# Eight experts' weights streamed through TensorE on one core: another order of the experts, four more places for weights, another tail

## The chip, the cores and the metric

The kernel runs on one core of a Trainium2 chip. The metric is the device time of one execution in microseconds (us). Everything is computed and stored in 32-bit floating point; the weights come from the chip's memory in that form.

## What is computed

Two transformer blocks over 256 tokens of width 1024. The change touches the last layer of the second block: a mixture of experts (each token goes to 2 of 8 SwiGLU experts, whose hidden width is 3584), and the gate behind it (PLE below, after its names in the code).

```python
def swiglu(x, w1, w3, w2):
    return (jax.nn.silu(x @ w1) * (x @ w3)) @ w2

def moe_swiglu(x, router_w, w1, w3, w2):
    logits = (xt @ router_w).astype(jnp.float32)
    top_vals, top_idx = lax.top_k(logits, TOP_K)
    gates = jax.nn.softmax(top_vals, axis=-1)
    ...
    for e in range(N_EXPERTS):
        out = out + combine[:, e:e + 1] * swiglu(xt, w1[e], w3[e], w2[e])

# the last layer
h = h + moe_swiglu(f, router_w[j], moe_w1[j], moe_w3[j], moe_w2[j])
gate = jax.nn.sigmoid(rmsnorm(h, ple_norm_g[i]) @ ple_gate_w[i])
h = h + gate * (p[i] @ ple_proj_w[i])
```

## The kernel before

**Steps.** An expert's hidden width is cut into four chunks, 1024, 1024, 1024 and 512 (CHUNKS, L33). A *step* is one expert and one chunk: the products with w1 and w3 of this step, and then the product with w2 of the step before, whose hidden values are ready by then. STEPS (L49) is the order of the 32 steps: experts 0 and 4 take turns chunk by chunk, then 1 and 5, 2 and 6, 3 and 7. The order is written out when the program is built; all engines follow it.

**The stream of weights** (_Stream, from L62). All matrices of the stage are cut into parts of 128 x 1024 numbers (512 KB), 24 for a full step, 12 for one of the short last chunk, 672 in all; then two parts of p's projection and eight of the gate's matrix (pg). SyncE sends a part (L89) as soon as a slot is free. There are 32 lasting slots: 8 (RAW), 8 tiles that the dense layers used for split weights (wh, wl), 6 (MORE) and 10 (EARLY). Seven more tiles (two x, then xl, xh, xl, x and gain) take one part each while they wait for their own use: load_parts. Parts of p and pg are split into a high and a low half first (split, L311 to L322: ScalarE the high half, VectorE or GpSimd the low one), and at most four split parts are live at a time (advance).

**A matrix on TensorE** (wide, from L1470). Each expert has room for its first 64 tokens, 32 more and 32 more. The product of the first 64 (mm for w1, s for w3, o for w2) goes over the parts as they come. The two others stand behind branches on the number of the expert's tokens (`If` at L1492, over 64, and L1495, over 96). They run as `rest`, put off until the first part of the *next* matrix is done (catch_up), and only after them all parts of the matrix are given back:

```python
            for j, _ in parts:
                self.ws.release(j)
            take(1)
        for i, (j, (k0, k1, _, _)) in enumerate(parts):
            if i == 1:
                self.catch_up()
```

With these inputs expert 1 has over 96 tokens, expert 2 between 65 and 96, the others 64 or fewer.

**Between the products.** At fixed parts of w1 and w3 stand: the transposes of the hidden values of the step before (hidden), the gather of the next expert's tokens (gather), and, for an expert that has just ended, its way back to the tokens' order (way_back) and the sum into h, weighted by the gates (scatter, with a branch at L1589 and the sum on VectorE at L1593).

**The tail.** experts() ends with: w2 of (3, 3), way_back and scatter of expert 3, hidden of (7, 3), way_back of expert 7, w2 of (7, 3). moe() then plays the product of p with its projection (ple_value, four groups) and scatters expert 7 between them, transposes the normed sum, and comes to a branch for experts with over 128 tokens (overflow, L1664 to L1666: all engines load the largest number and compare it). Behind it stands the gate's product with pg in two halves, and the output.

Of the kernel before, what the change touches and what calls it, by code (L numbers as in the profile page):

```python
# [48 lines left out]
STEPS = [(e, c) for e0 in range(NE // 2) for c in range(NC) for e in (e0, e0 + NE // 2)]  # L49
# [13 lines left out]
class _Stream:  # L63
# [3 lines left out]
    def __init__(self, net, plan):  # L67
        self.net, self.plan = net, plan
        self.parts = [(i, q, s) for i, c in enumerate(plan) for q, s in enumerate(c[4])]
        self.raw, self.got = {}, {}  # L70
        self.loaded = self.opened = self.cut = self.used = self.cur = self.first = self.live = 0
        self.slots, self.cap = [(net.wp, "raw", RAW)] * RAW, RAW
        self.extra, self.hold = set(), False

        self.last, self.keep = sum(len(c[4]) for c in plan[-3:]), None
# [29 lines left out]
    def load_parts(self, tiles):  # L105

        for tile in tiles:
            assert self.loaded == self.opened + self.cap
            self.extra.add(self.loaded)
# [3 lines left out]
    def open(self, u):  # L113
        self.opened += 1
        self.cap -= u in self.extra
        self.load()

    def advance(self, n=PARTS):
        stop = self.cut + n
        while self.cut < stop and self.cut < len(self.parts) and self.live < PARTS:  # L120
            u = self.cut
            if u not in self.raw or self.whole(u):
# [3 lines left out]
            f = self.net.split_pair if len(self.plan[i][4]) == 1 else lambda v: self.net.split(v, j)  # L126
# [71 lines left out]
class _Net:  # L198
# [112 lines left out]
    def split(self, v, j=0):  # L311

        k, n = v.shape[1], v.shape[2]
        wh = self.t(self.wp, [P, 1024], "wh", F32R, bufs=PARTS)[:, : k * n].rearrange("p (k n) -> p k n", k=k)
        wl = self.t(self.wp, [P, 1024], "wl", F32R, bufs=PARTS)[:, : k * n].rearrange("p (k n) -> p k n", k=k)
# [1043 lines left out]
    def ple_value(self, i, xs, pp):  # L1359

        out = self.banks("mm")
        order = [(0, 0), (1, 0), (0, 1), (1, 1)]
# [173 lines left out]
    def hidden(self, sp, s, n):  # L1536


        g = self.t(sp, [P, 2, 4, P], "sw_g")
# [7 lines left out]
    def down(self, key, ys, g, n, many, first):  # L1547
# [15 lines left out]
        self.wide(key, y, lhs, 512, many, take)  # L1563
# [4 lines left out]
    def scatter(self, t, e, back, ys, many=None):  # L1568

        ps = []  # L1570
        rows = [slice(SET * j, SET * j + SET) for j in range(2)]

        def first():
            ps[:] = [self.bank("tr") for _ in range(2)]
            for j in range(2):
                self.mm(ps[j], back[rows[j], 0, t * P : t * P + P], ys[rows[j], 0, :], start=True, stop=True, skip_group_check=True)

        def others():
            for i in range(2):
                for d in range(2):  # L1580
                    for j in range(2):
                        self.mm(ps[j][:, d * 256 : d * 256 + 256], back[rows[j], 1 + 2 * i + d, t * P : t * P + P],
                                ys[rows[j], 1, i * 256 : i * 256 + 256], start=False, stop=i == 1, skip_group_check=True)

        def second():
            if many is None:
                others()
            else:
                with self.tc.If(many() > SET):  # L1589
                    others()  # L1590
            for j in range(2):
                hv = self.h[:, t, j * 512 : j * 512 + 512]
                self.nc.vector.scalar_tensor_tensor(hv, ps[j], self.gates[:, t, e : e + 1], hv, ALU.mult, ALU.add)  # L1593
# [3 lines left out]
    def experts(self, sp, p):  # L1597
# [11 lines left out]

        def hidden(e, c, s):  # L1610
            gs[e, c] = self.hidden(sp, s, CHUNKS[c][1] // 2)

        def finish(e, c):
# [3 lines left out]
            self.down(("w2", e, c), ys[e], gs.pop((e, c)), CHUNKS[c][1] // 2, F(number, e), c == 0)  # L1617
            return e if c == NC - 1 else None

        for i, (e, c) in enumerate(STEPS):  # L1620
# [18 lines left out]
            if n < 512:  # L1639
                assert not late  # L1640
                mids = {k: mids.get(2 * k, []) + mids.get(2 * k + 1, []) for k in range(4)}
# [18 lines left out]
        return [f for t in range(NT) for f in self.scatter(t, x, back[x], ys[x], F(number, x))], pT  # L1660

    def overflow(self, sp, again):

        nc = self.nc  # L1664
        most = nc.values_load(self.most[0:1, 0:1], min_val=0, max_val=S)
# [32 lines left out]
    def route_join(self, gen):  # L1698
# [8 lines left out]
        self.stream.load_parts([t_(self.act, [P, D], "x", bufs=3) for _ in range(2)])  # L1707
# [38 lines left out]
        for tag in ("wh", "wl"):  # L1746
# [23 lines left out]
        self.stream.load_parts([t_(self.act, [P, D], tag, bufs=3) for tag in ("xl", "xh", "xl")]  # L1770
                               + [t_(self.act, [P, D], "x", bufs=3), t_(self.cst, [P, D], "gain")])
        self.next_gain()
# [42 lines left out]
    def moe(self, i):  # L1815
        sp = self.se
        p = self.ple_load(i, self.act, "x", 3)
        done, pT = self.experts(sp, p)
        pp = [self.t(self.act, [P, D], "x", bufs=3) for t in range(NT)]
        value = self.ple_value(i, pT, pp)  # L1820
        x0, *x0T = (self.t(self.qp, [P, D], "raw", bufs=EARLY) for _ in range(3))
        x0T = [x.bitcast(F32R).rearrange("p (k n) -> p k n", k=KD) for x in x0T]
        self.play(value, n=2)
        done[0]()
        done[1]()
# [117 lines left out]
```

## Time and profile before

| | us |
|---|---|
| runs | 1774.54, 1767.98, 1769.01 |
| median | 1769.01 |
| the profiled execution | 1774.91 |
| its span, first to last instruction | 1773.1 |
| TensorE busy in the span | 1652.7 (93%) |
| VectorE busy | 671.5 (38%) |
| ScalarE busy | 514.1 (29%) |

The profile is that of one execution. PE is TensorE (PEld its loads of the stationary operand, PEq its sequencer), DVE VectorE, ACT ScalarE, POOL GpSimd, SP SyncE (SPq its DMA queue). Numbers behind L are lines of the kernel. TensorE's clock has two levels, 1.2 and 2.4 GHz; the granted clock is the share of the higher one. In brackets behind a row of the timeline stands the engine's idle time before it and what ended it.

### The profile page before, as it was taken

To read this page: it belongs to the slowest core of one execution; us is meant where nothing else is said; L and a number is where in the kernel's file an instruction comes from. 1 tells how busy PE (TensorE), PEld (TensorE's weight loads), DVE (VectorE), ACT (ScalarE), POOL (GpSimd) and SP (SyncE) were. 2 spreads that over 40 slices of the span, in tenths; PEclk is the share of its full clock that TensorE was granted. 3 is DMA by queue.
4 is the path that set the end of the run, shared out by engine and by line. 5 is a ranking of instruction groups with operands and counts; after the bars stand their busy time and mean duration, and the time that the engine had idled before them with its cause. 6 is when DMAs were issued, how large, how long until landed. Compare 5 with 4: busy or idle time off the path is not lost. (4 is left out here: it accounts for less than half of the span.)

```text
span 1773.1 us, 24424 instructions
## 1 busy us (share of the span) xinstructions
PE 1652.7 (93%) x9746; PEld 1014.6 (57%) x9749; DVE 671.5 (38%) x1132; ACT 514.1 (29%) x840; POOL 158.4 (9%) x152
## 2 busy tenths in 40 slices
PE   8999989999999999999997999999999998998867
PEld 6887768777888877784332534336433344333336
DVE  6656767576445587571110130101120111311134
ACT  5646646555444455551100100000000001000013
POOL 2001432510000013500000000000000000000011
PEclk9999999999999999999999999999999999998979
DMA  8654335545555558567999998999789999999951
GB/s 272 201 175 146 108 95 168 180 122 185 182 187 190 190 163 292 194 250 308 406 407 399 400 393 306 406 357 401 283 320 374 408 397 404 370 407 407 397 207 38
DMA packets 176117, 491.70 MB, mean 277 GB/s; under 512 B 16670, under 2 KB 21206, under 8 KB 175920
## 3 DMA queue, kind: packets, MB, share of 16 engines
q1 hardware_dynamic: 171376, 474.28, 72.1%
q0 software_dynamic: 4544, 14.52, 2.8%
q8 instruction: 157, 2.57, 0.6%
q14 instruction: 40, 0.33, 0.0%
HBM read 486.60 MB, written 2.14 MB: 276 GB/s over the span
## 5 line engine op out<-in xcount | busy, mean ns | idle before, releaser
L272 PE MATMUL mm<-wh,xh 128*128 128x512 f32 (+4 forms) x888 | 324.0, 432 | 7.1 <-PEq L1492 4.0
L320 DVE TENSOR_TENSOR wl<-raw,wh 128x1024 fp32r<-128x1024 f32 x211 | 266.7, 1275 | 130.8 <-ACT wh L316 120.4
L272 PE MATMUL mm<-wh,xl 128*128 128x512 f32 (+1 forms) x704 | 281.4, 400 | 0.7 <-DVE xl L491 0.5
L316 ACT CAST wh<-raw 128x1024 fp32r<-128x1024 f32 x228 | 237.5, 1051 | 143.8 <-PE mm L272 68.2
L272 PE MATMUL mm<-wl,xh 128*128 128x512 f32 (+3 forms) x924 | 254.1, 416 | 1.2 <-DVE wl L320 0.6
L272 PE MATMUL mm<-raw,xh 128*64 128x512 f32 (+3 forms) x1388 | 201.2, 467 | 20.7 <-PEq L1492 14.2
L272 PE MATMUL o<-raw,sw_g 128*64 128x512 f32 (+1 forms) x1268 | 195.5, 503 | 16.7 <-PEq L1492 9.7
L272 PE MATMUL s<-raw,xh 128*64 128x512 f32 (+3 forms) x1432 | 193.4, 457 | 16.5 <-PEq L1492 12.4
L1532 DVE TENSOR_TENSOR sw_s<-sw_s,s 128x512 f32<-128x512 f32 (+1 forms) x64 | 39.8, 621 | 405.9 <-PE s L272 367.6
L272 PEld LDWEIGHTS mm<-wh,xh 128*128 128x128 f32 (+2 forms) x888 | 145.7, 180 | 54.4 <-issue 10.6
L272 PEld LDWEIGHTS mm<-wl,xh 128*128 128x128 f32 (+2 forms) x924 | 145.1, 175 | 51.5 <-issue 10.1
L272 PEld LDWEIGHTS mm<-wh,xl 128*128 128x128 f32 x704 | 134.9, 192 | 29.8 <-DVE xl L491 2.5
L318 POOL TENSOR_TENSOR wl<-raw,wh 128x1024 fp32r<-128x1024 f32 x17 | 43.0, 2549 | 1198.4 <-ACT wh L316 1178.4
L272 PEld LDWEIGHTS s<-raw,xh 128*64 128x64 f32 (+1 forms) x1432 | 77.0, 125 | 124.2 <-issue 80.9
L1544 ACT COPY sw_g<-tr 128x512 f32<-128x512 f32 (+1 forms) x32 | 17.1, 533 | 446.9 <-PE tr L275 425.8
L272 PEld LDWEIGHTS o<-raw,sw_g 128*64 128x64 f32 (+1 forms) x1268 | 72.0, 126 | 128.8 <-issue 95.8
L272 PEld LDWEIGHTS mm<-raw,xh 128*64 128x64 f32 (+1 forms) x1388 | 72.3, 127 | 119.0 <-issue 91.8
L1557 DVE TENSOR_TENSOR xl<-xl,o 128x512 f32<-128x512 f32 x48 | 33.0, 686 | 163.3 <-PE o L272 137.2
L1530 ACT ACTIVATE sw_s<-mm 128x512 f32<-128x512 f32 (+1 forms) x64 | 34.8, 544 | 206.0 <-PE mm L272 167.8
L272 PE MATMUL o<-wh,sw_g 128*128 128x512 f32 (+2 forms) x256 | 61.0, 488 | 3.8 <-PEq L1492 2.2
L272 PE MATMUL s<-wh,xh 128*64 128x512 f32 (+6 forms) x236 | 51.0, 467 | 3.3 <-PEq L1492 2.6
L275 PEld LDWEIGHTS tr<-c_ident,sw_s 128*128 128x128 f32 x280 | 34.0, 151 | 32.8 <-issue 9.1
(363 smaller groups left out, 1606.7 us busy)
## 6 DMA issues: line engine op xcount, KB each, us to landing
raw<-in_moe_w_dram SPq DMA_DIRECT2D x504, 512.0 KB, 10.2
raw<-in_dense_w_dram SPq DMA_DIRECT2D x84, 512.0 KB, 4.5
wh<-in_moe_w_dram SPq DMA_DIRECT2D x81, 512.0 KB, 10.2
wl<-in_moe_w_dram SPq DMA_DIRECT2D x80, 512.0 KB, 10.2
raw<-in_w_in_dram SPq DMA_DIRECT2D x48, 512.0 KB, 4.6
raw<-in_nsa_w_in_dram SPq DMA_DIRECT2D x44, 512.0 KB, 5.1
raw<-in_w_o_dram SPq DMA_DIRECT2D x16, 512.0 KB, 4.8
raw<-in_ple_gate_w_dram SPq DMA_DIRECT2D x16, 512.0 KB, 5.0
```

What stands on the lines that cost most here:

```text
L272: self.nc.tensor.matmul(out, lhsT, rhs, start=start, stop=stop, **kw)
L275: self.nc.tensor.transpose(out, in_, self.ident if ident is None else ident)
L316: self.nc.scalar.copy(wh, v)
L318: self.nc.gpsimd.tensor_tensor(wl, v, wh.bitcast(F32), ALU.subtract)
L320: self.owed.append(lambda: self.nc.vector.tensor_sub(wl, v, wh.bitcast(F32)))
L1530: nc.scalar.activation(s[:, i, :n], ps[i][:, :n], AF.Silu)
L1532: nc.vector.tensor_mul(s[:, i, :n], s[:, i, :n], ps[i][:, :n])
L1544: copy(g[:, i, : n // P, :], ps[:, :n].rearrange("p (q n) -> p q n", n=P))
L1557: self.nc.vector.tensor_add(ys[:, i, :], ys[:, i, :], y[i])
```

## The change

The experts no longer go in pairs. Each begins when its predecessor is half through, in the order 0, 4, 1, 5, 2, 6, 3, 7: the steps are 0c0, 0c1, 4c0, 0c2, 4c1, 0c3, 1c0, 4c2, 1c1, 4c3, 5c0, 1c2, and so on to 7c0, 3c2, 7c1, 3c3, 7c2, 7c3. Four of the seven tiles that took one part (three x and gain) become lasting slots, 36 in all. For that, p gets a tile of its own, the gate's gain is loaded in the last step instead of at the routing, and the gain's tile leaves the slots 34 parts before the stream's end.

In the tail, way_back and scatter of expert 3 and way_back of expert 7 move into w1 and w3 of the last step, and hidden of (7, 3) into w2 of (7, 2); w2 of (7, 3) follows at once. The first group of p's product stands between that product and its catch_up. Expert 7 is scattered into four banks with one branch, and its sums stand between the groups of p and behind the transposes. The number for the overflow branch is loaded earlier. Behind that branch two parts of pg's first half and two of its second are split at once; six split parts may be live at the stream's end.

```diff
-STEPS = [(e, c) for e0 in range(NE // 2) for c in range(NC) for e in (e0, e0 + NE // 2)]
+ORDER = [e for e0 in range(NE // 2) for e in (e0, e0 + NE // 2)]
+STEPS = [(ORDER[i], c) for _, c, i in sorted((2 * i + c, c, i) for i in range(NE) for c in range(NC))]
...
-            if len(self.parts) - self.loaded <= self.last and slot[0] is not self.keep and slot[:2] != (self.net.wp, "raw"):
+            left = len(self.parts) - self.loaded
+            if left <= self.last and slot[:2] != (self.net.wp, "raw") or slot[0] is self.net.cst and left <= self.last + 24:
                 self.cap -= 1
                 continue
...
     def open(self, u):
         self.opened += 1
         self.cap -= u in self.extra
+        if u in self.become:
+            self.slots.insert(0, self.become[u])
         self.load()
...
+            end = len(self.parts) - u <= self.last
+            if self.live >= PARTS + 2 * end:
+                break
...
+        if more:
+            wh, wl = (self.t(self.qp, [P, 1024], "raw", bufs=EARLY).bitcast(F32R) for _ in range(2))
...
+    def spread(self, ps, t, back, ys):
+        for j in range(2):
+            r = slice(SET * j, SET * j + SET)
+            self.mm(ps[j], back[r, 0, t * P : t * P + P], ys[r, 0, :], start=True, stop=True, skip_group_check=True)
...
+            if i == len(STEPS) - 1:
+                late[3] = [F(turn_back, e)]
+                self.next_gain()
             self.up(("w1", e, c), xT[e], s, n, F(number, e), True, mids)
             self.up(("w3", e, c), xT[e], s, n, F(number, e), False, late)
-            done = finish(*prev[:2]) if prev is not None else None
+            if i < len(STEPS) - 1:
+                done = finish(*prev[:2]) if prev is not None else None
+            else:
+                finish(*prev[:2], {4: [F(hidden_last, e, c, s)]})
...
-        self.catch_up()
-        back[done], turn = self.way_back(sp, done)
-        turn()
-        hidden(*prev)
-        for t in range(NT):
-            for f in self.scatter(t, done, back[done], ys[done], F(number, done)):
-                f()
-        x = prev[0]
-        back[x], turn = self.way_back(sp, x)
-        turn()
-        finish(*prev[:2])
-        self.catch_up()
+        self.stream.wait()
+        self.stream.advance(2)
+        finish(*prev[:2])
+        self.stream.advance(4)
+        value = self.ple_value(1, pT, pp)
+        self.play(value, n=1)
+        self.catch_up()
+        self.sets.pop("s")
+        ps = [[self.bank(tag) for _ in range(2)] for tag in ("tr", "s")]
         for t in range(NT):
+            self.spread(ps[t], t, back[e], ys[e])
+        with self.tc.If(number(e) > SET):
+            for t in range(NT):
+                self.spread_rare(ps[t], t, back[e], ys[e])
...
-        p = self.ple_load(i, self.act, "x", 3)
+        p = self.ple_load(i, sp, "p")
...
+        most = self.nc.values_load(self.most[0:1, 0:1], min_val=0, max_val=S)
         done[0]()
+        self.scaled(0, x0, (0,))
+        self.play(value, n=1)
         done[1]()
-        self.scaled(0, x0)
+        self.scaled(0, x0, (1,))
         self.play(value, n=1)
-        done[2]()
-        done[3]()
         self.transposed(x0, x0T, 0, 4)
         self.play(value)
         self.transposed(x0, x0T, 4, 8)
-        self.overflow(sp, lambda: self.transposed(self.scaled(0, x0), x0T))
+        done[2]()
+        done[3]()
+        self.overflow(sp, most, lambda: self.transposed(self.scaled(0, x0), x0T))
+        self.stream.advance(4)
```

How the instructions of TensorE move is shown at three places. The first is the start of the seventh step, of the kernel before: behind the last part of w2 of the step before (o, from the hidden values sw_g) comes the first part of w1 (mm, from the tokens' tile xh), and then the branch for the tokens over 64. xh_6764 holds the tokens of expert 0.

```order
L272 MATMUL o_7223<-wl_8235,sw_g_8343 64x512 x2
L272 MATMUL o_7223<-raw_8237,sw_g_8343 64x512 x2
L272 MATMUL mm_6826<-raw_8324,xh_6764 64x256 x4
L1492 COMPARE_AND_BRANCH
L272 MATMUL o_7224<-wh_8223,sw_g_8343 32x256 x4
L272 MATMUL o_7224<-wh_8225,sw_g_8343 32x256 x4
L272 MATMUL o_7224<-wh_8227,sw_g_8343 32x256 x4
```

The same place in the changed kernel, where the lines have moved by 10 to 15 and xh_8265 holds the tokens of expert 1.

```order
L282 MATMUL o_7211<-raw_8133,sw_g_8353 64x512 x2
L282 MATMUL o_7211<-raw_8135,sw_g_8353 64x512 x2
L282 MATMUL mm_6820<-raw_8137,xh_8265 64x512 x2
L1507 COMPARE_AND_BRANCH
L282 MATMUL o_7212<-raw_8024,sw_g_8353 32x256 x4
L282 MATMUL o_7212<-raw_8026,sw_g_8353 32x256 x4
L282 MATMUL o_7212<-raw_8028,sw_g_8353 32x256 x4
```

The step in this place is the short last chunk of expert 0 before (64x256), and the first chunk of expert 1 now; before, expert 1 begins two steps later.

The second place is TensorE's work between w2 of (3, 3) and w2 of (7, 3) in the kernel before: the way back of expert 3 (tr from oh), hidden of (7, 3) (tr from sw_s), the scatter of expert 3 (tr from xl and back).

```order
L275 MATMUL tr_16792<-c_ident_86,oh_2308_16785 128x128 x2
L275 MATMUL tr_16791<-c_ident_86,oh_2308_16785 128x128 x4
L275 MATMUL tr_16803<-c_ident_86,sw_s_16480 128x128 x2
L275 MATMUL tr_16807<-c_ident_86,sw_s_16480 128x128 x2
L272 MATMUL tr_16811<-xl_14831,back_16790 128x512
L272 MATMUL tr_16812<-xl_14831,back_16790 128x512
L1589 COMPARE_AND_BRANCH
L272 MATMUL tr_16811<-xl_14831,back_16790 128x256
L272 MATMUL tr_16812<-xl_14831,back_16790 128x256
```

In the changed kernel these stand in w3 and w2 of the last step. The piece is w2 of (7, 2), with hidden of (7, 3) in its middle; its last row is the first part of w2 of (7, 3), from the tile that hidden has filled.

```order
L282 MATMUL o_7211<-raw_16259,sw_g_16514 64x512 x2
L282 MATMUL o_7211<-raw_16261,sw_g_16514 64x512 x2
L282 MATMUL o_7211<-raw_16263,sw_g_16514 64x512 x2
L285 MATMUL tr_16762<-c_ident_86,sw_s_16466 128x128 x2
L285 MATMUL tr_16766<-c_ident_86,sw_s_16466 128x128 x2
L282 MATMUL o_7211<-raw_16265,sw_g_16514 64x512 x2
L282 MATMUL o_7211<-raw_16267,sw_g_16514 64x512 x2
L282 MATMUL o_7211<-raw_16269,sw_g_16514 64x512 x2
L282 MATMUL o_7211<-raw_16364,sw_g_16514 64x512 x2
L282 MATMUL o_7211<-raw_16366,raw_16761 64x512 x2
L1507 COMPARE_AND_BRANCH
```

What stood alone between two products stands inside one now, and the first part of the last product follows with nothing between. The third place is what comes behind that product in the changed kernel: the rest of its parts, p's first group (mm from wh and wl), and only then the branch for tokens over 64.

```order
L282 MATMUL o_7211<-raw_16368,raw_16761 64x512 x2
L282 MATMUL o_7211<-raw_16370,raw_16761 64x512 x2
L282 MATMUL o_7211<-raw_16372,raw_16761 64x512 x2
L282 MATMUL mm_16885<-wh_16867,xh_16177 128x512
L282 MATMUL mm_16885<-wh_16867,xl_16178 128x512
L282 MATMUL mm_16885<-wh_16867,xh_16177 128x512
L282 MATMUL mm_16885<-wh_16867,xl_16178 128x512
L282 MATMUL mm_16885<-wl_16868,xh_16177 128x512 x2
L1507 COMPARE_AND_BRANCH
```

Before, p's first group comes behind this branch.

## Rows read from the trace of the kernel before

**Rows 1.** Windows: start:end, length, busy us (instructions) by engine, PEclk, DMA share, GB/s.

```profile
920.00:998.00 78.00, 62.97 (x332) 26.87 (x330) 9.34 (x17) 5.45 (x11) 0.00 (x0) 0.93 1.03 400
...
1060.00:1253.00 193.00, 186.12 (x1826) 87.12 (x1824) 19.66 (x32) 11.97 (x22) 0.00 (x0) 0.99 0.95 371
1253.00:1360.00 107.00, 101.24 (x768) 41.67 (x766) 21.43 (x38) 6.89 (x12) 0.00 (x0) 1.00 0.81 307
...
1598.00:1689.00 91.00, 72.00 (x338) 29.17 (x336) 12.29 (x19) 5.88 (x11) 0.00 (x0) 0.90 1.03 402
...
1700.00:1726.00 26.00, 19.72 (x52) 7.42 (x52) 11.02 (x22) 3.21 (x4) 4.65 (x2) 0.61 0.35 124
```

**Rows 2.** Waits of SyncE's queue, 803 to 1689: us in total, times, longest.

```profile
SPq L89 <- PEq L1492: 96.6, 30, 15.7
SPq L89 <- PEq L1495: 53.5, 8, 15.3
```

**Rows 3.** Timeline of TensorE: first parts of w1 at the starts of steps.

```profile
998.50 1.06 PE L272 MATMUL mm<-wl,xh 128*64 128x512 f32 x4
...
1068.41 1.45 PE L272 MATMUL mm<-raw,xh 128*64 128x512 f32 x4
...
1112.19 1.03 PE L272 MATMUL mm<-raw,xh 128*64 128x512 f32 x4
...
1550.63 1.06 PE L272 MATMUL mm<-wh,xh 128*64 128x512 f32 x4
...
1575.12 1.06 PE L272 MATMUL mm<-raw,xh 128*64 128x512 f32 x4
```

**Rows 4.** Page, DMA issues: KB each, median us from issue to landing.

```profile
wh<-in_moe_w_dram SPq DMA_DIRECT2D x81, 512.0 KB, 10.2
```

**Rows 5.** Timeline of SyncE's queue: the last weight of an expert.

```profile
1688.56 0.33 SPq L89 DMA_DIRECT2D wh<-in_moe_w_dram  x1
```

**Rows 6.** Timeline of TensorE, 1700 to 1726.

```profile
1700.04 4.49 PE L272 MATMUL o<-raw,sw_g 128*64 128x512 f32 x12 [2.16 <-DMA raw<-in_ple_proj_w_dram]
...
1709.83 0.69 PE L275 MATMUL tr<-c_ident,sw_s 128*128 128x128 f32 x2 [0.51 <-ACT sw_g L1544]
...
1714.04 2.73 PE L272 MATMUL tr<-xl,back 64*128 64x512 f32 x4 [0.94 <-DVE h L1593]
...
1720.45 4.96 PE L272 MATMUL o<-raw,sw_g 128*64 128x512 f32 x12
1725.24 1.02 PE L272 MATMUL o<-wh,sw_g 128*64 128x512 f32 x4
```

**Rows 7.** Timeline of VectorE in the tail: the gain, and two gated sums.

```profile
1732.88 1.68 DVE L463 TENSOR_TENSOR raw<-h,gain 128x512 f32<-128x512 f32 x2
1734.48 1.40 DVE L1593 SCALAR_TENSOR_TENSOR h<-tr,gates,h 128x512 f32<-128x512 f32 x2
```

**Rows 8.** Timeline, all engines, around the overflow branch.

```profile
1738.07 2.34 POOL L318 TENSOR_TENSOR wl<-raw,wh 128x1024 fp32r<-128x1024 f32 x1 [4.66 <-ACT wh L316]
...
1740.84 0.49 PE L272 MATMUL mm<-wh,raw 128*128 128x512 f32 x1 [3.06 <-ACTq L1666]
...
1742.57 1.65 PE L272 MATMUL mm<-wh,raw 128*128 128x512 f32 x3 [1.24 <-DVEq L1666]
```

**Rows 9.** Waits of TensorE, 803 to 1700: us in total, times, longest.

```profile
PE mm L272 <- PEq L1492: 18.4, 12, 5.1
PE s L272 <- PEq L1492: 16.3, 24, 5.6
PE o L272 <- PEq L1492: 12.2, 9, 2.8
PE tr L275 <- PEq L1492: 5.2, 1, 5.2
```

**Rows 10.** Timeline of TensorE: two waits for the branch.

```profile
964.72 5.39 PE L272 MATMUL s<-raw,xh 128*64 128x256 f32 x24 [5.60 <-PEq L1492]
...
1632.16 1.98 PE L272 MATMUL mm<-raw,xh 128*64 128x512 f32 x4 [5.14 <-PEq L1492]
```

More of the change, by code (lines that the diff above doesn't have):

```diff
@@ L72, in __init__ @@
         self.slots, self.cap = [(net.wp, "raw", RAW)] * RAW, RAW
-        self.extra, self.hold = set(), False
-        self.last, self.keep = sum(len(c[4]) for c in plan[-3:]), None
+        self.extra, self.become, self.hold = set(), {}, False
+        self.last = sum(len(c[4]) for c in plan[-3:])
     def whole(self, u):
@@ L103, in load, with load_parts @@
                 between.pop(0)()
-    def load_parts(self, tiles):
+    def load_parts(self, tiles, slot=None):
         for tile in tiles:
             assert self.loaded == self.opened + self.cap
-            self.extra.add(self.loaded)
+            if slot:
+                self.become[self.loaded] = slot
+            else:
+                self.extra.add(self.loaded)
             self.load_part(tile)
@@ L119, in advance @@
         stop = self.cut + n
-        while self.cut < stop and self.cut < len(self.parts) and self.live < PARTS:
+        while self.cut < stop and self.cut < len(self.parts):
             u = self.cut
+            end = len(self.parts) - u <= self.last
+            if self.live >= PARTS + 2 * end:
+                break
             if u not in self.raw or self.whole(u):
@@ L1361, in ple_value @@
         out = self.banks("mm")
+        if pp[0] is None:
+            pp[:] = [self.t(self.act, [P, D], "x", bufs=3) for _ in range(NT)]
         order = [(0, 0), (1, 0), (0, 1), (1, 1)]
@@ L1608, in number, with turn_back, hidden_last, finish @@
             return tokens[e]
+        def turn_back(e):
+            back[e], turn = self.way_back(sp, e)
+            turn()
+        def hidden_last(e, c, s):
+            g = self.t(self.qp, [P, 1024], "raw", bufs=EARLY).rearrange("p (i q n) -> p i q n", i=2, q=4)
+            gs[e, c] = self.hidden(sp, s, CHUNKS[c][1] // 2, g)
         def hidden(e, c, s):
             gs[e, c] = self.hidden(sp, s, CHUNKS[c][1] // 2)
-        def finish(e, c):
+        def finish(e, c, mids=None):
             if c == 0:
                 ys[e] = self.results()
-            self.down(("w2", e, c), ys[e], gs.pop((e, c)), CHUNKS[c][1] // 2, F(number, e), c == 0)
+            self.down(("w2", e, c), ys[e], gs.pop((e, c)), CHUNKS[c][1] // 2, F(number, e), c == 0, mids)
             return e if c == NC - 1 else None
@@ L1647, in experts, with overflow @@
                 pT = self.ple_T(p)
+        self.stream.wait()
[4 more added lines that the diff above has]
+        self.play(value, n=1)
         self.catch_up()
-        back[done], turn = self.way_back(sp, done)
-        turn()
-        hidden(*prev)
+        self.sets.pop("s")
+        ps = [[self.bank(tag) for _ in range(2)] for tag in ("tr", "s")]
         for t in range(NT):
-            for f in self.scatter(t, done, back[done], ys[done], F(number, done)):
-                f()
-        x = prev[0]
-        back[x], turn = self.way_back(sp, x)
-        turn()
-        finish(*prev[:2])
-        self.catch_up()
-        return [f for t in range(NT) for f in self.scatter(t, x, back[x], ys[x], F(number, x))], pT
-    def overflow(self, sp, again):
+            self.spread(ps[t], t, back[e], ys[e])
+        with self.tc.If(number(e) > SET):
+            for t in range(NT):
+                self.spread_rare(ps[t], t, back[e], ys[e])
+        return value, [F(self.add_gated, t, j, e, ps[t][j]) for t in range(NT) for j in range(2)]
+    def overflow(self, sp, most, again):
         nc = self.nc
-        most = nc.values_load(self.most[0:1, 0:1], min_val=0, max_val=S)
         with self.tc.If(most > CAP):
@@ L1706, in route_join @@
         sq = [self.sq_tile() for _ in range(NT)]
-        self.stream.load_parts([t_(self.act, [P, D], "x", bufs=3) for _ in range(2)])
+        self.stream.load_parts([t_(self.act, [P, D], "x", bufs=3) for _ in range(2)], (self.act, "x", 3))
         junk = t_(self.act, [P, D], "x", bufs=3)
```

63 lines of the change are left out of this document (32 added, 31 removed).

## The prediction, before the changed kernel was run

> **What bounds the kernel now.** I read the stages first, then the waits of the DMA queue and of TensorE, then single stretches in order of time, and last the tail.
>
> The windows [rows 1] show who is ahead of whom. From 920 to 998 us and again from 1598 to 1689 the DMA moves 400 and 402 GB/s, and a part of 512 KB (524,288 bytes) takes 524,288 / 402,000 = 1.30 us; TensorE is busy for only 62.97 of 78 us (920 to 998) and 72.00 of 91 (1598 to 1689). From 1060 to 1360 it is the other way round: TensorE is busy 287 of 300 us and the DMA falls to 371 and then 307 GB/s. So the expert stage is bound by the transfers at both of its ends and by TensorE in its middle. SyncE says the same: to send the next part it waited 96.6 us for the branch after which a matrix's slots are released, and 53.5 us for the branch of the third group of tokens [rows 2].
>
> Why the middle is slow can be read from the starts of steps [rows 3]: from one w1 to the next w1 an ordinary step takes 1575.12 - 1550.63 = 24.5 us and a step of expert 1 takes 1112.19 - 1068.41 = 43.8. A full step has 24 parts, 24 x 1.30 = 31.2 us of DMA. Ordinary steps wait for weights, those of expert 1 leave the DMA ahead until all slots are full.
>
> The DMA's idle time in the middle, counted against 402 GB/s, is 193 x (1 - 371/402) = 14.9 us and 107 x (1 - 307/402) = 25.3: together 40 us. TensorE's lost time before it is 78 - 62.97 = 15.0 us, and its granted clock of 0.93 there (mostly the 2.4 GHz level, the lower one after idle time) is worth 0.07 x 63 = 4.4 more: 19.4.
>
> In the tail nothing hides. The last expert weight is issued at 1688.56 and, with the page's median of 10.2 us to landing [rows 4, 5], is there at 1698.8. The last product of expert 7 ends at 1725.24 + 1.02 = 1726.3 [rows 6], 27.5 us later, and from there to the end of the span are 1773.1 - 1726.3 = 46.8 us.
>
> **The change, part by part.**
>
> *Order.* Nothing is removed: the same 32 steps and 672 parts. What moves is expert 1's extra work, from the ninth step to the seventh. Parts ahead of its first w1: 164 before (w1 and w3 of eight steps, 112, w2 of seven, 52), now 128 (88 and 40). That is 36 parts, 36 x 1.30 = 46.8 us sooner, about 952 instead of 998.5 [rows 3], inside the stretch in which TensorE starves. The starving spared is at most 19.4 x 46.8 / 78 = 11.6 us. Every step of expert 1 alternates with an ordinary one as before, and such a pair takes TensorE 43.8 + 24.5 = 68.3 against 62.4 us of DMA, so the lead comes back slowly, 5.9 us in a pair. I take **-10.0**. Bounds: 0 (the starving only moves) and -40 (all idle time of the DMA).
>
> *Four more places for weights.* The parts that these four tiles hold first are sent in both kernels; afterwards the change uses the tiles again, the kernel before does not. From 920 to 998 that gives nothing, since the transfers bind there [rows 1]. In the middle SyncE stops when all slots are full, now four parts later, and the stretch at the end that the transfers bind begins with four parts more in hand: 4 x 1.30 = **-5.2**. Bounds: 0 (the middle is bound by TensorE's work and the lead is used up by it) and -10.4 (it shortens the idle time of both slow stretches, 1060 to 1253 and 1253 to 1360). They cost no instruction.
>
> *The gain's load, p in a tile of its own, the constants' slot given up 34 parts early.* One DMA each, or none. The gain goes out on GpSimd's queue in the last step; GpSimd is idle from 1598 to 1689 [rows 1] and VectorE reads the gain first at 1732.88 [rows 7]. The cover is the last step, over 40 us; without it a load like the others, 10.2 us [rows 4], would stand before the gate. Zero, and 0 to +2 for the slot.
>
> *Way back and scatter of expert 3, way back of expert 7, hidden part of the last step.* They stand between 1704.53 (end of w2 of expert 3) and 1720.45 (start of the last w2) [rows 6]: 15.9 us. TensorE's work there is its 19.72 us from 1700 to 1726 [rows 1] less 4.49 and 5.6 for the two products: 9.6 us, at a granted clock of 0.61. Now they are in the last step and the w2 after it, while parts are still landing. What remains is TensorE's lag behind the DMA: w2 of expert 3 ended at 1704.5, its last part landed four parts before the end, 1698.8 - 5.2 = 1693.6, so 10.9 us; with two times the hidden transposes (0.69 for half of them) 12.3 instead of 27.5: **-15.2**. Bounds: the last 16 parts are 20.8 us of DMA and some 15 us of products, which leaves 6 us for 9.6, so 4 us may come back (-11); with a lag of 8 it is -19. Late next is the product itself, behind the last part.
>
> *The rest of the tail.* Before, TensorE stood 3.06 + 1.24 = 4.3 us at the overflow branch [rows 8], in front of which each engine loads the number that it compares; that load now stands before the last product of p. The scatter of expert 7 has four banks instead of two, so its second pair no longer stands behind VectorE as that of expert 3 did for 0.94 us [rows 6]. Against that, two gated sums, 1.40 us together [rows 7], now stand after the transposes, on VectorE just before the branch, and the splits of the second half's parts are issued after it: 2.34 us each for the low half where GpSimd makes it [rows 8], beside the products of the parts ahead of them. I take **-2.0**, bounds +1.5 and -4.3.
>
> Sum: -10.0 - 5.2 - 15.2 - 2.0 = -32.4. The profiled execution took 1774.9 us (its span 1773.1); it lies 5.9 above the median of the runs, 1769.0. So 1774.9 - 32.4 = 1742.5 under the profile and 1742.5 - 5.9 = **1736.6** as a median.
>
> *A rule against it.* The rows that speak against a thin lead are TensorE's waits for its own sequencer after the test on the number of tokens: 46 in the stage, 18.4 + 16.3 + 12.2 + 5.2 = 52.1 us, 1.1 on average, but 5.1 to 5.6 at worst [rows 9]. The two shown, of 5.60 and 5.14 us, lie where the transfers bind [rows 10]. I leave their sum unchanged. The Trainium skill, "Runtime: NRT & Kernel Launch", section "Instruction fetch mechanics", says that a taken branch to a target outside the pages already fetched stops the engine until that page has come by DMA. By that rule every skipped group would pay such a stall, whatever the lead; the trace agrees only in part, since most of the 96 tests cost far less than 5 us.
>
> **Rivals.**
>
> *Only the tail pays.* What expert 1 saves by coming early it gives back where experts 1 and 2 follow one another; the DMA idles as long as before, only sooner. For it: SyncE's waits come in blocks of eight slots, and the lead is gone before expert 1 starts in either order. Then -15.2 - 2.0 = -17.2: 1774.9 - 17.2 - 5.9 = 1751.8.
>
> *Nearly all idle transfers go.* With 36 slots and expert 1 starting on an empty lead, its four pairs gain 4 x 5.9 = 23.6 us of lead and could hold 28 parts, 36 us: the queue would never be full. Three quarters of the 40 us and the four places, -30 - 5.2 - 17.2: 1716.6. Against it: the releases come eight at a time, after the product of the next matrix has begun.
>
> *Slower: the branches take it.* Expert 1's and 4's steps now run with an empty lead while the DMA is saturated, and each test there costs as much as the worst ones. From 893 to 1000 there are some 14 tests (107 us are four to five steps with three tests each). At 5.2 us each instead of 1.1 they cost 14 x 4.1 = 57 us; 57 - 32.4 = +25, 1774.9 + 25 - 5.9 = 1794. It decides from ten of them on (10 x 4.1 = 41, 8.8 us more than is won). Against it: from 920 to 998 of the kernel before, with the lead just as empty, only one wait reached 5 us [rows 10]. This is what the rule above would do if it held for every skip with the transfers saturated.
>
> *Nothing.* The last step has no room for the moved work, and the lag grows by what the tail loses; order and places are hidden. Then 1765 to 1769.
>
> **How the numbers follow.** Forecast 0.60 (its own range 1723 to 1748: the order term between 0 and -20, the tail between its bounds); only the tail 0.17; nearly all 0.11; slower 0.07; nothing 0.05. A measurement of this kernel tells 0.5%, 8.8 us, from no change. Faster by more (below 1760.2): 0.60 + 0.17 + 0.11 = 0.88; same 0.05; slower 0.07. The range 1714 to 1757 takes in the first three but for the fast edge of the third, and leaves out the last two.
>
> **Signs.** Right: w1 of expert 1 starts near 952; TensorE idles under 8 us from there to 1000; 1060 to 1360 has 390 GB/s or more; the last expert weight is issued near 1673; the last w2 ends about 12 us after its last part lands, and the span ends 45 us after that. If the last weight still goes out at 1688, the order and the places are worth nothing; if the last w2 ends 20 us or more behind the landing, the moved work has only moved; if the waits on the test sum to over 90 us, the branches have taken it.

## The result, and the profile after

| | us |
|---|---|
| changed kernel, median of 4 runs (1748.3 to 1753.2) | 1750.9 |
| kernel before, in the same rounds | 1768.5 |
| ratio | 0.990 (0.9865 to 0.9931) |
| the same two in a second comparison (6 and 13 runs) | 1746.1 and 1767.6 |
| its ratio | 0.989 (0.986 to 0.992) |
| profiled execution of the changed kernel, and its span | 1751.3, 1749.5 |

Faster by 1.0%, 18 to 22 us, where 32 were forecast. Windows of the changed kernel (columns as in [rows 1]):

```profile
920.00:998.00 78.00, 74.64 (x568) 33.37 (x566) 14.07 (x26) 5.87 (x11) 0.00 (x0) 0.98 1.03 407
1060.00:1253.00 193.00, 179.79 (x1608) 80.91 (x1608) 27.61 (x49) 11.96 (x22) 0.00 (x0) 0.97 0.91 347
1253.00:1360.00 107.00, 99.16 (x696) 43.79 (x696) 16.60 (x29) 7.04 (x13) 0.00 (x0) 0.98 0.95 364
1360.00:1489.00 129.00, 119.71 (x866) 51.33 (x864) 21.86 (x37) 9.43 (x17) 0.00 (x0) 0.99 1.00 390
```

TensorE is idle 3.4 us from 920 to 998 instead of 15.0 [rows 1]. The idle transfers of the middle did not go, they spread: 193 x (1 - 347/402) = 26.4 us, 10.1 and 3.9, 40 us in all, as many as before (14.9 and 25.3). The same in longer windows, of the kernel before and then of the changed one:

```profile
1060.00:1489.00 429.00, 404.56 (x3508) 181.80 (x3506) 56.62 (x96) 28.45 (x52) 0.00 (x0) 1.00 0.94 365
1489.00:1680.00 191.00, 170.84 (x828) 67.23 (x826) 34.67 (x58) 14.76 (x26) 0.00 (x0) 0.96 1.01 396
```

```profile
1060.00:1489.00 429.00, 398.67 (x3166) 176.03 (x3166) 66.07 (x115) 28.42 (x52) 0.00 (x0) 0.98 0.94 364
1489.00:1680.00 191.00, 168.81 (x856) 70.69 (x855) 36.30 (x62) 15.45 (x29) 0.56 (x1) 0.97 1.03 402
```

So the transfers gained nothing in the middle, and 191 x 6/402 = 2.9 us behind it. The largest gain stands at the very start: in the 20 us from the last part of the first fill on they move 286 GB/s (801 to 821) instead of 204 (799 to 819), which is 20 x 82/402 = 4.1 us. From there to 1060 it is 404 instead of 400, 2.4 us more.

The timeline of SyncE's queue gives the stage's length, from the last part of the first fill (into the gain's tile) to the last weight of an expert. Before, with its end in [rows 5]:

```profile
799.30 0.33 SPq L89 DMA_DIRECT2D gain<-in_moe_w_dram  x1
```

After:

```profile
801.15 0.33 SPq L90 DMA_DIRECT2D gain<-in_moe_w_dram  x1
...
1680.98 0.33 SPq L90 DMA_DIRECT2D raw<-in_moe_w_dram  x1
```

The stage took 1688.56 - 799.30 = 889.3 us before and 879.8 now, 9.5 us less. Note the start: 799.3 and 801.2 here, 789.5 to 802.9 over the traces below, in a part of the program that no edit touched. A single span carries that difference, the stage's length does not.

What the start of the stage gains can be read from the same queue. Before, TensorE's first w1 held the gather of expert 4's tokens, 16 products twice (the first row, and one like it at 810.76), and the next part went out 17.7 us after the gain's:

```profile
807.77 2.05 PE L272 MATMUL tr<-oh,f 128*128 128x128 f32 x16
...
817.00 3.84 SPq L89 DMA_DIRECT2D raw<-in_moe_w_dram  x8
```

In the changed kernel expert 4 begins one step later and its gather is out of this matrix. The next part goes out 13.3 us after the gain's:

```profile
814.43 9.00 SPq L90 DMA_DIRECT2D raw<-in_moe_w_dram  x12
```

The tail, timeline of all engines:

```profile
1695.94 1.08 PE L282 MATMUL o<-raw,raw 128*64 128x512 f32 x4 [0.84 <-issue]
...
1697.17 2.79 PE L282 MATMUL o<-raw,raw 128*64 128x512 f32 x12 [0.15 <-PEq L1507]
...
1714.03 2.37 PE L282 MATMUL mm<-wh,raw 128*128 128x512 f32 x4 [3.10 <-ACTq L1704]
...
1715.43 5.69 POOL L331 TENSOR_TENSOR raw<-raw,raw 128x1024 fp32r<-128x1024 f32 x2 [7.67 <-ACT raw L329]
...
1717.28 4.92 DVE L333 TENSOR_TENSOR wl<-raw,wh 128x1024 fp32r<-128x1024 f32 x2 [3.64 <-ACT wh L329]
...
1722.12 1.28 DVE L476 TENSOR_TENSOR f<-h,gain 128x512 f32<-128x512 f32 x2
1722.95 0.63 PE L285 MATMUL tr<-c_ident,f 128*128 128x128 f32 x4 [3.13 <-DVE f L476]
```

The last w2 ends at 1697.17 + 2.79 = 1700.0. With 10.2 us to landing the last weight is there at 1691.2, so the lag (from there to the end of the last w2) is 8.8 us instead of 27.5. The wait at the overflow branch is 3.10 us (4.3 before, in two pieces [rows 8]). New is a wait of 3.13 us for VectorE's normed sum (f), which stands behind two splits of 2.46 us each; GpSimd splits beside it, 2.85 us each where one took 2.34 [rows 8].

TensorE's waits behind the test, 803 to 1700, answer to [rows 9]:

```profile
PE o L282 <- PEq L1507: 16.3, 19, 3.4
PE mm L282 <- PEq L1507: 12.4, 8, 4.1
PE s L282 <- PEq L1507: 10.2, 21, 2.6
...
PE tr L285 <- PEq L1507: 2.8, 1, 2.8
```

41.7 us in 49 waits, where there were 52.1 in 46.

### The profile page after: what moved, and what is told of

The parts are those of the page before. It is cut to its first block, busy times and chain, and to the rows that moved or that the text cites. A ratio compares the mean times of both kernels' runs of the same rounds, so it can differ in the third digit from the quotient of the medians.

```text
span 1749.5 us, 24548 instructions
## 1 busy us (share of the span) xinstructions
PE 1645.0 (94%) x9749; PEld 1017.8 (58%) x9749; DVE 676.7 (39%) x1132; ACT 513.9 (29%) x840; POOL 157.8 (9%) x152
## 3 DMA queue, kind: packets, MB, share of 16 engines
q8 instruction: 157, 2.57, 0.6%
## 5 line engine op out<-in xcount | busy, mean ns | idle before, releaser
L282 PE MATMUL mm<-wh,xh 128*128 128x512 f32 (+5 forms) x996 | 325.0, 415 | 7.7 <-PEq L1507 2.4
L282 PE MATMUL mm<-wl,xh 128*128 128x512 f32 (+2 forms) x840 | 248.0, 422 | 3.5 <-PEq L1507 2.7
L282 PE MATMUL mm<-raw,xh 128*64 128x512 f32 (+3 forms) x1236 | 184.9, 475 | 13.0 <-PEq L1507 7.3
L282 PE MATMUL o<-raw,sw_g 128*64 128x512 f32 (+1 forms) x1132 | 173.8, 501 | 16.0 <-PEq L1507 13.3
L282 PE MATMUL s<-raw,xh 128*64 128x512 f32 (+3 forms) x1016 | 158.7, 484 | 15.2 <-PEq L1507 6.9
L282 PEld LDWEIGHTS o<-raw,sw_g 128*64 128x64 f32 (+1 forms) x1132 | 64.8, 126 | 114.4 <-issue 74.4
L282 PEld LDWEIGHTS mm<-raw,xh 128*64 128x64 f32 (+1 forms) x1236 | 67.0, 127 | 107.7 <-issue 66.6
L282 PEld LDWEIGHTS s<-raw,xh 128*64 128x64 f32 (+1 forms) x1016 | 61.9, 130 | 104.7 <-issue 74.3
L331 POOL TENSOR_TENSOR wl<-raw,wh 128x1024 fp32r<-128x1024 f32 x15 | 37.9, 2545 | 402.5 <-ACT wh L329 382.5
L282 PE MATMUL s<-wh,xh 128*64 128x512 f32 (+6 forms) x364 | 58.8, 439 | 0.7 <-PEq L1507 0.3
## 6 DMA issues: line engine op xcount, KB each, us to landing
raw<-in_moe_w_dram SPq DMA_DIRECT2D x454, 512.0 KB, 10.2
wh<-in_moe_w_dram SPq DMA_DIRECT2D x72, 512.0 KB, 10.1
wl<-in_moe_w_dram SPq DMA_DIRECT2D x72, 512.0 KB, 10.1
x<-in_moe_w_dram SPq DMA_DIRECT2D x54, 512.0 KB, 10.1
gain<-in_moe_w_dram SPq DMA_DIRECT2D x17, 512.0 KB, 10.2
```

The costliest lines, as they stand in the source:

```text
L282: self.nc.tensor.matmul(out, lhsT, rhs, start=start, stop=stop, **kw)
L331: self.nc.gpsimd.tensor_tensor(wl, v, wh.bitcast(F32), ALU.subtract)
```

## Experiments

All are edits of the changed kernel. "To before" is the difference to the median of the kernel before in the same rounds, in us; "ratio, 95%" is the interval of the ratio to it; "stage" is the length as above from the one trace of each. Single executions of one kernel spread over 5 to 18 us; differences under 5 us are not told from none.

| run | median | to before | ratio, 95% | stage |
|---|---|---|---|---|
| e5, the changed kernel again | 1746.1 | -21.5 | 0.986 to 0.992 | 874.7 |
| e1, 32 slots | 1747.2 | -20.2 | 0.986 to 0.992 | 880.1 |
| e2, experts in pairs | 1745.8 | -21.7 | 0.985 to 0.991 | 879.9 |
| e3, both undone | 1756.5 | -10.9 | 0.992 to 0.996 | 886.2 |
| e4, splits later | 1741.1 | -26.4 | 0.982 to 0.987 | 877.1 |
| e8, pairs, splits later | 1746.3 | -21.3 | 0.985 to 0.991 | 884.5 |
| e6, 28 slots | 1754.9 | -12.8 | 0.991 to 0.997 | 894.8 |
| e7, no tests | 1680.5 | -87.2 | 0.949 to 0.955 | 823.6 |
| e9, no tests, 28 slots | 1692.3 | -77.7 | 0.953 to 0.958 | 839.4 |
| e10, no tests, e3's order and slots | 1694.4 | -75.6 | 0.954 to 0.960 | 837.6 |
| e11, two short tests | 1768.0 | -2.3 | 0.996 to 1.000 | 895.4 |
| e12, one test for two matrices | 1778.3 | +7.7 | 1.003 to 1.007 | 913.1 |

### Order and places apart: e1, e2, e3, e5

e1 takes the four tiles once only:

```diff
-        self.stream.load_parts([t_(self.act, [P, D], "x", bufs=3) for _ in range(2)], (self.act, "x", 3))
+        self.stream.load_parts([t_(self.act, [P, D], "x", bufs=3) for _ in range(2)])
...
-        self.stream.load_parts([t_(self.cst, [P, D], "gain")], (self.cst, "gain", 1))
+        self.stream.load_parts([t_(self.cst, [P, D], "gain")])
```

> The changed kernel with the four places used once only, as before (32 lasting slots). The changed kernel took 1750.9 us, and its last expert weight went out about 7.5 us sooner than before, where I had forecast 15.2. Theory A: the places give the 5.2 us forecast, the order the small rest: 1756, and the last weight goes out 5 us later than in the changed kernel. Rival B: the order gave all of it and the places nothing, because the idle transfers of the middle come from the release of eight slots at a time: 1751. Rival C: the places gave all of it: 1758 to 1759.

e2 puts six experts in pairs again:

```diff
-STEPS = [(ORDER[i], c) for _, c, i in sorted((2 * i + c, c, i) for i in range(NE) for c in range(NC))]
+PAIRS = [(e, c) for e0 in range(3) for c in range(NC) for e in (e0, e0 + NE // 2)]
+STEPS = PAIRS + [(ORDER[i], c) for _, c, i in sorted((2 * i + c, c, i) for i in (6, 7) for c in range(NC))]
```

> The changed kernel with the first six experts in pairs again (0 and 4, 1 and 5, 2 and 6); only 3 and 7 stay staggered, so the new tail stays whole, and so do the four places. Theory A: the order is worth only 2 to 3 us: 1753 to 1754. Rival B: it is worth 7 to 8: 1758 to 1759. Rival C: nothing: 1751. In all three TensorE idles again some 15 us from 920 to 1000 us.

e3 makes both edits, e5 none.

> Both undone, the tail alone. If the parts add up, the last weight goes out where it did before (1688 us of the span) and the time is 1758 to 1759 under every theory, 10 us under the kernel before: the tail's share. If it is over 1763, tail and order don't add.

> The changed kernel itself, timed in the same rounds as the next three, because single executions of these kernels spread over 8 to 14 us and its first comparison had few. Order alone gave 1747 and the places alone 1746, from 1756.5 for the tail alone. If both do the same thing (fill the queue once, so that the second finds nothing left to gain), the changed kernel lies with them at 1745 to 1750; if they add, it should be near 1737; if they hurt one another, above 1751.

The tail alone is worth 10.9 us. Order alone adds 9.3 to it (1756.5 to 1747.2), the places alone 10.8 (to 1745.8), both together 10.4 (to 1746.1), where the sum would be 20.1: in the medians, whichever is there first takes the gain. e3 came as expected; e1 and e2 came out below all three of their figures. None of the three theories of e1 and e2 had that: each gave the gain to one of the two, or let them add. The expectation of e5, written with e1 and e2 known, had it.

The stages say it less clearly: 887.8 as the mean of the two kernels with neither (before, e3), 880.1 with the order, 882.2 with the places (e2, e8), 877.2 with both (the two traces of the changed kernel and e4). That is -7.7, -5.6, and together -10.6 where the sum is -13.3, while traces of kernels with the same stage lie up to 5 us apart (874.7 to 879.8; 879.9 and 884.5).

That the order pays by sparing the starving is not shown. e2, in pairs, starves again, as expected:

```profile
920.00:998.00 78.00, 61.41 (x342) 29.27 (x338) 10.73 (x23) 5.22 (x11) 0.00 (x0) 0.93 1.03 401
```

But the order without the places is e1 against e3. The first 20 us of the stage and the stretch behind the middle, e1:

```profile
797.00:817.00 20.00, 18.84 (x87) 8.74 (x90) 1.79 (x11) 4.14 (x7) 0.00 (x0) 0.91 0.73 282
...
1489.00:1680.00 191.00, 165.13 (x850) 69.28 (x846) 38.86 (x69) 15.45 (x29) 0.00 (x0) 0.98 1.03 402
```

e3:

```profile
803.00:823.00 20.00, 19.36 (x102) 10.91 (x106) 1.93 (x11) 5.31 (x9) 0.00 (x0) 0.91 0.52 205
...
1489.00:1680.00 191.00, 172.91 (x862) 66.64 (x860) 38.16 (x67) 15.11 (x27) 0.00 (x0) 0.98 1.01 394
```

From the first 20 us to 1060 it is 400 GB/s in e1 and 402 in e3, from 1060 to 1489 367 in both. So the order's gain lies at the start and behind the middle, some 4 us each, and none of it where TensorE starved. The start goes with the order in every trace in which a matrix's slots hang on its own tests: 271 to 298 GB/s in the first 20 us with the new order (the changed kernel twice, e1, e4, e6, e11), 199 to 207 in pairs (before, e2, e3, e8). No run moves the gather by itself. Why order and places together give no more than one of them in the medians stays open.

### Fewer slots: e6

```diff
-MORE = 6
+MORE = 2
```

This is e1 with four slots of the MORE tiles taken away.

> The changed kernel with 28 lasting slots instead of 36. By my price of 5.2 us for four places: eight fewer cost 10.4 us, and half of it lies between 28 and 32. If the places only matter until the order has removed the starving, 28 costs under 3 us against 32 (1747): 1750. If each four are worth the 10.8 us that four were worth with the pairs, it is 1758 or more.

The time, 1754.9, lies between the two that I had set. 7.4 us for the four between 28 and 32, and none to be seen from 32 to 36 under this order (1.3), both as differences to before: the price seems to grow as slots get fewer, and my 5.2 lies between.

### The splits behind the overflow branch: e4, e8

```diff
-        self.stream.advance(4)
         xs = [x0T, self.new_xT()]
         x1 = self.scaled(1, self.t(self.rp, [P, NT, D], "f")[:, 1, :])
         sq = self.sq_tile()
         self.halves(sq[:, 0], 0, x0)
+        self.stream.advance(4)
```

> The changed kernel with its four splits of the gate's weights put behind the normed sum of the second half of the tokens, instead of straight behind the overflow branch. In the changed kernel TensorE idles 3.13 us there for VectorE's normed sum, which stands behind two splits of 2.46 us each. Theory: the sum comes first and 3 us go: 1748. Rival: the parts of the second half are then split too late and TensorE waits as long for them: 1750 to 1751.

> Pairs for the first six experts, the four places, the new tail, and the splits behind the normed sum: the two best results put together. If the order adds nothing to the places and the splits are worth what they seemed to be (4 to 9 us): 1737 to 1741, no slower than the changed kernel with later splits (1741). If the order matters beside the places, it is 3 us or more slower than that.

e4 has the lowest time of the kernels that hold for any inputs, 1741.1, below both of my figures, and beats the kernel before clearly. That it beats the changed kernel isn't shown: the intervals touch, and e8 is no faster than e2. By the limit that I had set for e8 (3 us above e4) the order matters beside the places, since e8 is 5.2 slower than e4; e2 and e5, the same two without the later splits, are 0.3 apart. Whether the order adds up to 5 us to the places is not told by these runs. e4's trace shows why little can be won: the 3.13 us are gone, and instead TensorE waits for the low half of the second tokens' tile:

```profile
1726.17 0.50 PE L282 MATMUL mm<-wh,xl 128*128 128x512 f32 x1 [2.40 <-DVE xl L504]
```

### What holds the middle up: e7, e9, e10

e7 decides when the program is built which experts run the later groups (key[1] is the expert):

```diff
-            with self.tc.If(many() > SET):
-                for j, (k0, k1, _, _) in parts:
-                    product(1, j, k0, k1)
-                with self.tc.If(many() > SET + SUB):
-                    for j, (k0, k1, _, _) in parts:
-                        product(2, j, k0, k1)
+            for s in range(1, 1 + {1: 2, 2: 1}.get(key[1], 0)):
+                for j, (k0, k1, _, _) in parts:
+                    product(s, j, k0, k1)
```

> The changed kernel without the tests on the number of tokens in the products: the groups over 64 are run for experts 1 and 2 and left out for the others when the program is built (this holds for these inputs only). TensorE's waits behind those tests sum to 42 us in the changed kernel, 19 of them between 998 and 1489, where TensorE is the bound. Theory: the middle is bound by TensorE, so those 19 us come off, and some 5 of the stall in the last step: 1725 to 1735. Rival: the transfers are the bound and the waits are covered: within 3 us of the changed kernel.

1680.5 us where 1725 to 1735 was expected: 65.6 less than the changed kernel in the same rounds. The windows of e7:

```profile
1060.00:1253.00 193.00, 192.68 (x1748) 84.96 (x1746) 31.48 (x54) 12.16 (x22) 0.00 (x0) 1.00 1.02 402
1253.00:1360.00 107.00, 106.68 (x759) 47.10 (x756) 20.65 (x37) 9.08 (x17) 0.00 (x0) 1.00 1.03 406
1360.00:1489.00 129.00, 126.52 (x800) 51.66 (x800) 21.83 (x39) 10.61 (x21) 0.00 (x0) 1.00 1.03 407
```

Here the transfers never stop, TensorE hardly idles, and the granted clock is 1.00. The pages of the changed kernel and of e7 show two more things: TensorE's busy time, and the instruction queue. The changed kernel:

```profile
PE 1645.0 (94%) x9749; PEld 1017.8 (58%) x9749; DVE 676.7 (39%) x1132; ACT 513.9 (29%) x840; POOL 157.8 (9%) x152
...
q8 instruction: 157, 2.57, 0.6%
```

e7:

```profile
PE 1617.7 (96%) x9749; PEld 984.1 (59%) x9749; DVE 671.8 (40%) x1132; ACT 511.2 (30%) x840; POOL 157.7 (9%) x152
...
q8 instruction: 80, 1.31, 0.3%
```

The same 9749 products take 27 us less (17 less than in e5, whose trace has TensorE busy for 1634.2). The granted clock is 0.97 to 0.99 in the first windows of the changed kernel above, where TensorE was idle at tests, and 1.00 in those of e7. Its mean over the span is 0.977 in the changed kernel, 0.983 in e5 and 0.993 in e7, and busy time times clock gives 1607, 1606 and 1606 us: by this estimate the clock bears all of the difference. So a wait costs more than its own row says. And skipped instructions are fetched all the same: with tests the queue moves 2.57 MB, without 1.31.

A test also keeps the eight slots of its matrix until it is decided. e9 is e7 with e6's 28 slots, e10 is e7 with e3's order and slots.

> No tests on the number of tokens, as in the run without branches (1680), and 28 lasting slots instead of 36. A test costs in two ways: TensorE waits behind it, and the eight slots of its matrix are given back only after it, since the products behind it may still read them. Taking eight slots away puts the second back in number. Theory A: what counts is the eight slots held: 1715 to 1750. Theory B: what counts is that TensorE no longer stops and no slot's release hangs on a branch; 28 free slots are enough to keep the transfers going: 1680 to 1690.

> No tests, the first six experts in pairs and 32 lasting slots: of the change only the tail. Theory: order and places are worth something only because the tests let the transfers stop; without tests the transfers never stop and this takes as long as the run without tests that has both, 1680, within 3 us. Rival: order and places are worth their 10 us here too: 1690.

Eight slots fewer cost 11.8 us in the medians (1680.5 to 1692.3) and 9.5 in the differences to before: between my two theories, nearer to the second. If that is what holding eight slots costs, the other 54 to 56 of the 65.6 us are the stops and the clock lost with them. e10 refutes my theory on the change: without tests, order and places are worth 14.0 us by the medians and 11.6 by the differences to before, not nothing. In both the transfers stop in one only of the three stretches of the middle, that in which expert 1's work ends and expert 2's begins. e9:

```profile
1060.00:1253.00 193.00, 192.68 (x1699) 84.37 (x1699) 30.52 (x53) 13.63 (x25) 0.00 (x0) 1.00 0.98 383
```

e10:

```profile
1060.00:1253.00 193.00, 193.00 (x1852) 90.45 (x1846) 25.96 (x46) 12.61 (x24) 0.00 (x0) 1.00 0.96 373
```

e7, with the new order and 36 slots, moves 402 GB/s there. So without tests order and places together bridge the surplus of work, which they did not do with them (347 and 364). What they are worth is the same either way within the noise: 11.6 us without tests and 10.6 with them (e3 to e5), as differences to before.

### Can the tests be had cheaper: e11, e12

e11 puts the second test behind the first:

```diff
-                with self.tc.If(many() > SET + SUB):
-                    for j, (k0, k1, _, _) in parts:
-                        product(2, j, k0, k1)
+            with self.tc.If(many() > SET + SUB):
+                for j, (k0, k1, _, _) in parts:
+                    product(2, j, k0, k1)
```

> The changed kernel with the test for more than 96 tokens behind the one for more than 64 instead of inside it: an expert of 64 or fewer takes two tests to a matrix, each skipping 128 instructions of TensorE (64 products and their loads), where it now skips over 256 at once. Nothing else changes, and nothing hangs on these inputs. Theory: the price of a test, some 53 of the 66 us between the changed kernel and the one without tests, is the wait for instructions behind a long skip, as the Trainium skill's rule on taken branches has it (Runtime: NRT & Kernel Launch, section Instruction fetch mechanics); a short skip stays in what is already there: 1690 to 1715, and TensorE's waits behind the first test fall from 42 us to under 10. Rival: each test has a price of its own, whatever it skips; twice as many tests cost more: 1765 to 1800.

By the differences to before, 15 to 19 us slower than the changed kernel. TensorE's waits behind the last of the two tests:

```profile
PE o L282 <- PEq L1510: 24.1, 25, 2.6
PE s L282 <- PEq L1510: 19.9, 23, 4.0
PE mm L282 <- PEq L1510: 18.6, 17, 2.9
PE tr L285 <- PEq L1510: 6.4, 7, 2.7
```

69.0 us in 72 waits, 0.96 each, where the changed kernel had 0.85: halving the skip did not shorten the wait, and there are more of them. The theory fell; the rival's range (1765 to 1800) holds the time.

e12 keeps w1's later groups until w3's and runs both under one test:

```diff
+        elif key[0] == "w1":
+            self.first_half = group, back
         else:
             self.late.append(rest)
```

where rest() runs group and gives back the slots for both halves.

> The changed kernel with one test for w1 and w3 of a step together, run behind the first part of the next w2: 64 tests on the products instead of 96, each skipping the groups of two matrices. The slots of w1 stay held until then, eight more for a third of the time. Theory A: each test has its own price, 53 us / 96 = 0.55 us (twice as many tests cost 18 us more); 32 fewer save 11 to 18 us, the slots held give back 4 to 12: 1735 to 1750. Theory B: what is paid is the skipped instructions, which are as many as before (the fetch queue moved 2.57 MB with tests and 1.31 MB without): no gain, and the slots cost 4 to 12: 1752 to 1762.

1778.3 us is slower than either theory had it; by the differences to before it is 25 to 29 us slower than the changed kernel. The waits behind its test:

```profile
PE o L282 <- PEq L1519: 55.0, 23, 3.6
...
PE mm L282 <- PEq L1519: 9.5, 9, 3.6
...
PE tr L285 <- PEq L1519: 2.8, 1, 2.8
```

67.3 us in 33 waits, 2.0 each, and most of them behind the double skip. Per test (waits by the number of tests) it is 0.43 us in the changed kernel, 0.36 in e11, 1.05 in e12. Read so, a skip has a price of its own and one that grows with what it skips. That is argued from three kernels and not shown: e12 also holds w1's slots longer. Of the three, the nested test per matrix has the lowest sum of waits and the lowest time. What the fetch does at a skip, the profile doesn't show; that stays open.

## Why the prediction was right, and where it was off

The direction held, and the time lies in the range (1714 to 1757). The size was off: 1736.6 forecast, 1750.9 measured, 14.3 us apart: 5.4 from the offset, 7.6 from the stage (9.5 us shorter instead of 15.2, and 1.9 later in starting), -3.5 from the lag and 4.7 from what follows it.

That the time lies in the range is in part luck: the order's term came near for another reason than the one I gave.

**The offset.** I took the profiled execution as 5.9 us above its median, and carried that over. The changed kernel's profiled one lies 0.5 above its own, and that of e5, the same kernel, 2.6 below (1743.4 and 1746.1). Under the profile 1742.5 was forecast and 1751.3 measured, so 5.4 of the 14.3 us are this step. The start of the stage alone moves by 13 us from trace to trace.

**Order and places, -10.0 and -5.2.** Expert 1 began at 945.7 (952 forecast), and 11.6 us of idle TensorE went from 920 to 998, as many as I had worked out as a bound. But the step from there to the time did not hold: the middle's transfers idle for as long as before, and what the order gains stands at the start of the stage, where the gather of expert 4 left the first matrix, and behind 1489. The prediction has no term for either. That the order alone is worth 9.3 us, against -10.0, is luck. For the places alone the mean stage is 5.6 us shorter, for -5.2, and the median 10.8 lower. The sum was an error too: the medians of both together show 10.4 us, the stages 10.6, where I had let the two add to 15.2. The rival "only the tail pays" had the middle right (the transfers idle as long as before, only sooner) and the rest wrong: its 1751.8 lies near the measured time by coincidence, since e3, the tail alone, takes 1756.5, 10.4 more than both together. The signs of 390 GB/s from 1060 to 1360 and of a last weight near 1673 failed with 347 and 364, and with 1681.0.

**The tail.** The lag fell to 8.8 us, 18.7 less where 15.2 were forecast: the moved work did fit into the last step. From the end of the last w2 to the end it took 49.5 us instead of 46.8, where I had forecast 2.0 less. Of the wait at the overflow branch 1.2 us went; the step that failed is the splits "beside the products of the parts ahead of them": VectorE's two splits held up the normed sum for 3.13 us. I had costed GpSimd's part of it and not what stands behind VectorE's. The traces give the tail more than the medians do: from the issue of the last weight to the end of the span it is 84.5 us before, 68.5 in the changed kernel and 69.1 in e3, 15 to 16 us less, where the medians of e3 show 10.9 and I had forecast 17.2. With one trace of the kernel before, itself 5.9 us above the median, it stays open which is nearer.

**The rivals.** "The branches take it" did not come: the waits summed to 41.7 us, not over 90, and TensorE, with expert 1 from 945.7 on, was busy 74.64 of the 78 us from 920 to 998. What the tests cost with all that follows from them e7 shows: 65.6 us. The Trainium skill, "Runtime: NRT & Kernel Launch", section "Instruction fetch mechanics", says that a taken branch to a target outside the pages fetched waits for a DMA. That every skip here is such a branch was my own step, and no run shows it. The conclusion that I drew from it, that a skip of half the length would be nearly free, e11 refutes. "Nearly all idle transfers go" needed what only e7 has.

## What to carry to other kernels

Two remedies for the same idle transfers need not add: work out the second on what the first leaves. A gain in one engine's idle time is not yet a gain in the stage: look in which windows the engine that bounds the stage moved more. A branch that skips work costs more than the wait in its row, through the slots held until it is decided and what else hangs on the stop; try the stage once without it before tuning around it. Measure a stage between two rows of the same trace rather than by the span, when the part ahead of it moves by more than the effect.

## What I had not expected

Taking 96 tests out of a stage of 880 us saved 65.6 us, where the waits listed behind them summed to 41.7. TensorE's busy time for the same 9749 products fell from 1645.0 (1634.2 in the second trace) to 1617.7 us with it. The instruction queue moved 2.57 MB with tests, whether they were nested, split or joined (2.57, 2.57 and 2.56), and 1.31 MB without: what is skipped is fetched. And the new order of the experts paid first of all at the start of the stage, where it takes a gather out of the first matrix, and not where TensorE had starved.
